# A hybrid RWKV/convolution block: a projection tile's products by halves of the contraction, not by quarters

## The chip, the cores and the metric

The kernel runs on one core of a Trainium2 chip. The metric is the device time of that core in microseconds for one execution. Lower is better. The engines are TensorE (PE in the profile; PEld is its loading of weights), VectorE (DVE), ScalarE (ACT), GpSimd (POOL) and SyncE (SP), which issues most transfers.

## The reference

One layer, one batch, 512 tokens of 2048 values with 16 meta tokens ahead of them:

```python
meta = jnp.broadcast_to(meta_tokens[None].astype(x.dtype), (bsz, N_META, D_MODEL))
h_res = jnp.concatenate([meta, x], axis=1)
hn = _rmsnorm(h_res, norm_in_g[l])
P = hn @ w_in[l]                        # (528 x 2048) @ (2048 x 8320)
Pr, Pc = P[..., :RW_COLS], P[..., RW_COLS:]
prev = jnp.pad(Pr[:, :-1], ((0, 0), (1, 0), (0, 0)))
Pr = Pr + (prev - Pr) * mu_shift[l]     # r, k, v, g_r and two narrow low-rank inputs
...
y = _rwkv7_recurrence(rh, decay, kh, vh, kk, kk * ah)   # 16 heads of 64, state carried over tokens
y_a = (yn + bonus) * jax.nn.silu(g_r)
Bg, Cg, hc, g_c = ...                   # four blocks of 1024 columns of Pc
y_b = Bg * _causal_depthwise_conv(Cg * hc, conv_w[l]) * jax.nn.silu(g_c)
h_res = h_res + jnp.concatenate([y_a, y_b], axis=-1) @ w_out[l]
out = _rmsnorm(h_res, norm_f_g)[:, N_META:]
```

The change concerns the first large product, `hn @ w_in`, alone.

## The kernel before, in words

**Tiles.** The projection is cut into 65 tiles of 128 output columns (`plan`). Each is a sum over 2048 rows, 16 blocks (`kt`) of 128. The first four tiles (`lora`, `k0`, `r0`, `B0`) are interleaved by a code of their own in `mains`; the other 61 are made one after the other by `main`. Their order is written out in `plan`, by pairs of head tiles: `k, r, v` of two neighbours, their `g`, and then one group `C, h, B, gc` of the convolution branch; from pair 4 on the order is the same, and the last four groups of the convolution branch come at the end, where the recurrence runs.

**Products.** All values are float32, split into a high and a low part of a shorter type. Each `kt` needs three products: high weight with low token part (`xl`), high weight with high token part (`xh`), and low weight with `xh`. A `B` or `gc` tile needs the 512 real tokens alone; it makes 48 products of 512 columns (`steps`). All others also need meta tokens: `k` and `v` tiles ("full") all 16, and `r`, `g`, `C`, `h` tiles ("tail") the last two. There the 512 tokens lie in two token pieces of 256, each in a PSUM bank of its own: the straight piece (r = 0) and the wide piece (r = 1). Copies of the meta tokens stand behind the real ones, and the wide piece reaches over them in its `xh` passes: a full tile's widths in the passes high·`xl`, high·`xh`, low·`xh` are 256, 288 and 274, a tail tile's 256, 260 and 258 (`WIDE`). That makes 96 products.

**Order inside a tile.** `pieces` (L343 to L356) goes by quarters of the contraction, four `kt` each: first the 12 straight products, `kt` by `kt`; then the 12 of the wide piece, pass by pass. The order of PE's instructions is that of the code; on the other engines a scheduler arranges them, with priorities (`ahead`, `high_priority`).

**Weights.** A tile's weights arrive in two transfers of 512 KB on SP's queue (`prefetch`, three raw buffers). Each is two quarters, and `split_w` makes the two parts of a quarter: a cast on ScalarE (L151) and a subtraction on VectorE (L152), "low part" below. The pool `hl` holds six quarters; a quarter's buffer is free for the next cast when the last product that reads it is done. `main` asks for two transfers a tile, one at its start and one ahead of the second quarter.

**Other work on PE.** The products of the recurrence's preparation (`prepare`, `invert`) and of the recurrence (`recur`) are put between projection products. `fill(ns)` lets the projection run on until its products have counted `ns`, and each product counts its width times 0.43. The same count (`clock`) releases deferred transfers (`later`, `run_pending`), SP's queue of stores and reloads among them. For a pair of heads, `prepare` makes the triangular products `gram` (L754) and, in `gram_meta`, a few narrow ones: key norms (L786), products with the meta tokens (L765) and, for the odd tile of a pair, the second level of a triangular inverse (`level_b`, L1023 and L1027). The narrow ones are written into the two PSUM banks of the projection tile that comes next (`next_banks`), ahead of its first product. VectorE empties them by two masks (L775) and eight copies (`take_b`, L1037), ScalarE by a copy of the norms. If the projection tile has counted more than 48 products at that point, `gram_meta` stands ahead of `gram`, otherwise behind it. In `invert`, the products `t0` (L961) read `xn`, a transpose (L946) on VectorE.

**Evictions.** At a tile's end VectorE scales its two banks into SBUF (`scaled`, L402, L403, L413), and ScalarE, VectorE and GpSimd finish it (shift by a token, gate, convolution).

Of the kernel before, what the change touches and what calls it, by code (L numbers as in the profile page):

```python
# [18 lines left out]
P = 128  # L19
DM = 2048  # L20
KT = DM // P
SEQ = 512
META = 16
# [66 lines left out]
def hymba_kernel(ctx: ExitStack, tc: tile.TileContext, xt, xtok, front, w_in, w_out, pv, lup, cst, msk, gf, out):  # L90
    nc = tc.nc
# [41 lines left out]
    quarters, chain, low = {}, {}, {}  # L133
    state = {"next": 0, "step": 0, "banks": []}
# [13 lines left out]
    def split_w(q, rq, eng):  # L148
        what, i, half = kind_of(q // 2)
        hi, lo = parts_of((what, i, half + q % 2), f"w{q}")  # L150
        nc.scalar.copy(hi, rq)  # L151
        low[q] = eng.tensor_tensor(out=lo, in0=rq, in1=hi.bitcast(F32), op=ALU.subtract).ins  # L152
        quarters[q] = (hi, lo)

    def prefetch(upto):
        while state["next"] < min(upto, len(stream) if chain else N_IN):
            j = state["next"]
            raw = chain[j - N_IN] if j >= N_IN else wp.tile([P, 1024], F32, tag="raw", name=f"wr{j}", bufs=3)
            state["dma"] = nc.sync.dma_start(raw, stream[j]).ins
            with tc.high_priority(offset=WEIGHTS):  # L160
                for q in range(2):
                    split_w(2 * j + q, raw[:, q * 512 : (q + 1) * 512], nc.vector)
            state["next"] = j + 1
# [6 lines left out]
    xh = xp.tile([P, KT, LX], F32R, name="xh")  # L170
    xl = xp.tile([P, KT, LX], F32R, name="xl")
# [159 lines left out]
    HALF, EX = META + SEQ // 2, 2 * META  # L331
    WIDE = {"full": (L + EX, L, L + META + 2), "tail": (L + 4, L, L + 2)}
# [7 lines left out]
            nc.scalar.copy(rsx[:, o : o + b - a], rs[:, a:b])  # L340
        nc.scalar.copy(rst, rsx[:, 0:4])

    def pieces(kind, ps, k4, q):  # L343
        hi, lo = quarters[q]
        for r in range(2):
            a = HALF if r else META
            ends = WIDE[kind] if r else (HALF,) * 3
            passes = ((hi, xl, ends[1]), (hi, xh, ends[0]), (lo, xh, ends[2]))
            for n, k in [(n, k) for n in range(3) for k in range(4)] if r else [(n, k) for k in range(4) for n in range(3)]:
                ww, xx, b = passes[n]  # L350
                kt = 4 * k4 + k
                nc.tensor.matmul(  # L352
                    ps[r][:, 0 : b - a], ww[:, k * P : (k + 1) * P], xx[:, kt, a:b], start=(kt == 0 and n == 0),
                    stop=(kt == KT - 1 and n == 2), skip_group_check=True,
                )
                yield (b - a) * 0.43  # L356

    def steps(ps, ranges, k4, q, ks=range(4), rs_=range(2)):
        hi, lo = quarters[q]
        for r, (a, b) in enumerate(ranges):  # L360
            if r not in rs_:
                continue
            for k in ks:
                kt = 4 * k4 + k
                w = slice(k * P, (k + 1) * P)
                for n, (ww, xx) in enumerate(((hi, xh), (hi, xl), (lo, xh))):
                    nc.tensor.matmul(  # L367
                        ps[r], ww[:, w], xx[:, kt, a:b], start=(kt == 0 and n == 0), stop=(kt == KT - 1 and n == 2)
                    )
                    yield (b - a) * 0.43  # L370

    def banks(ranges, name, pool, tag):
        return [pool.tile([P, b - a], F32, tag=tag, name=f"ps_{name}_{r}") for r, (a, b) in enumerate(ranges)]
# [5 lines left out]
    def main(j, ranges, name):  # L379
        prefetch(2 * j + 4)  # L380
        early = state["banks"]
        state.update(tile=j, step=0, banks=[])
        kind = ranges if isinstance(ranges, str) else None
        if kind:
            ranges = ((META, HALF), (HALF, WIDE[kind][0]))
        ps = [early[r][:, 0 : b - a] for r, (a, b) in enumerate(ranges)] if early else banks(ranges, name, pm, "main")
        for k4 in range(4):
            if k4 == 1:
                prefetch(2 * j + 5)
            for t in pieces(kind, ps, k4, 4 * j + k4) if kind else steps(ps, ranges, k4, 4 * j + k4):  # L390
                state["step"] += 1
                yield t
        return ps
# [149 lines left out]
    def mains():  # L543
# [35 lines left out]
        for j in range(4, len(plan)):  # L579
            what, i = plan[j]  # L580
            rg = "full" if what in ("k", "v") else REAL if what in ("B", "gc") else "tail"
            ps = yield from main(j, rg, f"{what}{i}")
            if (what, i) == ("h", 0):
                state["conv"] = low[4 * j + 6]
            if what == "gc" and i < 4:
                state["split"] = low[4 * j + 4]
            use(what, i, ps)
# [710 lines left out]
    for half in range(2):  # L1298
        units += [(half, "M1", g) for g in range(4)]
        units += [(half, prod, g) for g in range(4) for prod in ("P5", "M7", "M3", "Q6")]  # L1300
        ends = ("P4", 0), ("P4", 1), ("M2", 0), ("P4", 2), ("M2", 1), ("P4", 3), ("M2", 2), ("M2", 3)
# [156 lines left out]
    for half in range(2):  # L1458
        o = 28 * half
        for g in range(4):  # L1460
            b = o + 4 + 4 * g
# [51 lines left out]
    for u, unit in enumerate(units):  # L1513
        half, prod, g = unit
# [53 lines left out]
    with tc.manual_schedule(engines={mybir.EngineType.DVE, mybir.EngineType.Activation, mybir.EngineType.Pool}):  # L1568
# [15 lines left out]
        ends = [po.tile([P, 256], F32, tag="o", name=f"end{part}") for part in range(2)]  # L1584
        for part in range(2):
            cols = slice(256 * part, 256 * part + 256)
            for jj in range(8):
                hi, lo = right[(1, "M2", jj // 2), jj % 2]
# [75 lines left out]
```

## Time and profile before

| what | value |
|---|---|
| median of 3 runs | 993.13 us (991.97 to 993.62) |
| span of the profiled execution | 991.2 us |
| PE busy | 981.2 us, 99%, 9511 instructions |
| VectorE busy | 707.8 us, 71% |
| ScalarE busy | 390.4 us, 39% |
| GpSimd busy | 128.0 us, 13% |
| DMA, SP's main queue | 60.2% of 16 engines' span |
| moved | 176.89 MB, 178 GB/s over the span |
| TensorE's granted clock | full speed, 9 tenths or more in each of the 40 slices |

The page gives no time of its own for the profiled execution beside its span of 991.2 us. In the lists below a row has its start in us from the span's start, its duration in us, the engine, the line, the operation, output and inputs by the program's names without their numbers, the shapes, and how many instructions are merged into it; a bracket tells the idle time ahead of it and what ended that. Ends of products are modelled, starts are recorded. A row of the page's first two lists stands for the whole span.

### The profile page before, as it was taken

What the parts mean: (1) busy time and instruction counts of PE and PEld (TensorE: products, weight loads), DVE (VectorE), ACT (ScalarE), POOL (GpSimd) and SP (SyncE); (2) the same over time, 40 slices, a digit from 0 to 9 for tenths busy, and PEclk for the clock granted to TensorE, in tenths of its full rate; (3) what the DMA queues carried; (4) which work ended last, traced back from release to release, by engine and by line L of the source; (5) the groups of instructions that cost most, each with busy time, mean ns of one, the idle gap of its engine ahead of it and who ended that gap; (6) DMA issues with size and microseconds to landing.
All of it is one profiled execution on the core that took longest, in us unless ns stands there. A gap on an engine that the chain in (4) does not pass through costs nothing.

```text
span 991.2 us, 23393 instructions
## 1 busy us (share of the span) xinstructions
PE 981.2 (99%) x9511; PEld 907.4 (92%) x9511; DVE 707.8 (71%) x1413; ACT 390.4 (39%) x731; POOL 128.0 (13%) x242
## 2 busy tenths in 40 slices
PE   9999999999999999999999999999999999999996
PEld 8999999999998999998999998889889898788885
DVE  6777966578675679653779654465756697998897
ACT  7553432344322434322434323232332435546464
POOL 0110302012010121010111010011211102001001
PEclk9999999999999999999999999999999999999999
DMA  9526576246675385853375856988886697697654
GB/s 324 156 91 149 145 202 160 88 126 150 152 181 166 92 194 117 211 150 107 87 186 122 205 143 189 280 250 250 229 252 189 179 281 197 183 313 197 149 128 170
DMA packets 205387, 176.89 MB, mean 178 GB/s; under 512 B 138528, under 2 KB 168032, under 8 KB 204768
## 3 DMA queue, kind: packets, MB, share of 16 engines
q1 hardware_dynamic: 202688, 166.50, 60.2%
q0 software_dynamic: 2304, 8.39, 4.9%
q8 instruction: 74, 1.21, 0.5%
q10 hardware_dynamic: 288, 0.52, 0.1%
q14 instruction: 33, 0.27, 0.1%
HBM read 139.02 MB, written 36.35 MB: 177 GB/s over the span
## 4 chain that ended last, share of the span: by engine, by line
PE 94%; DVE 3%; DMA 1%; ACT 1%; issue 1%; SPq 0%; DVEq 0%; POOL 0%; ACTq 0%
PE ps_v L352 9%; PE ps_h L352 9%; PE ps_C L352 9%; PE ps_g L352 9%; PE ps_gc L367 9%; PE ps_B L367 9%; PE ps_k L352 8%; PE ps_r L352 8%; PE M L1381 5%; PE P L1381 4%; PE Q L1381 2%; PE g L754 2%; PE ps_lora L367 1%; PE ps_k L367 1%; PE zy L1139 1%; PE ps_r L367 1%
## 5 line engine op out<-in xcount | busy, mean ns | idle before, releaser
L151 ACT CAST w<-wr 128x512 fp32r<-128x512 f32 x252 | 153.7, 619 | 285.8 <-PE ps_C L352 47.5
L152 DVE TENSOR_TENSOR w<-wr,w 128x512 fp32r<-128x512 f32 x252 | 175.3, 707 | 117.7 <-ACT w L151 116.7
L352 PE MATMUL ps_v<-xh,w 128*128 128x256 f32 (+2 forms) x512 | 84.0, 285 | 0.0
L367 PE MATMUL ps_B<-xh,w 128*128 128x512 f32 x256 | 83.4, 394 | 0.0
L352 PE MATMUL ps_h<-xh,w 128*128 128x256 f32 (+2 forms) x512 | 81.6, 281 | 0.0
L352 PE MATMUL ps_g<-xh,w 128*128 128x256 f32 (+2 forms) x512 | 81.5, 281 | 0.0
L367 PE MATMUL ps_gc<-xh,w 128*128 128x512 f32 x256 | 81.1, 392 | 0.0
L352 PE MATMUL ps_C<-xh,w 128*128 128x256 f32 (+2 forms) x512 | 80.8, 280 | 0.0
L352 PEld LDWEIGHTS ps_v<-xh,w 128*128 128x128 f32 x512 | 73.9, 188 | 0.3
L352 PE MATMUL ps_k<-xh,w 128*128 128x256 f32 (+1 forms) x448 | 73.4, 285 | 0.0
L352 PE MATMUL ps_r<-xh,w 128*128 128x256 f32 (+1 forms) x448 | 72.6, 281 | 0.0
L352 PEld LDWEIGHTS ps_h<-xh,w 128*128 128x128 f32 x512 | 72.1, 189 | 0.3
L352 PEld LDWEIGHTS ps_g<-xh,w 128*128 128x128 f32 x512 | 72.0, 189 | 0.4
L352 PEld LDWEIGHTS ps_C<-xh,w 128*128 128x128 f32 x512 | 71.7, 189 | 0.2
L352 PEld LDWEIGHTS ps_k<-xh,w 128*128 128x128 f32 x448 | 64.7, 188 | 0.4
L352 PEld LDWEIGHTS ps_r<-xh,w 128*128 128x128 f32 x448 | 63.5, 189 | 0.2
L352 PE MATMUL ps_h<-xl,w 128*128 128x256 f32 x256 | 57.3, 281 | 0.0
L367 PEld LDWEIGHTS ps_gc<-xh,w 128*128 128x128 f32 x256 | 47.8, 188 | 10.0
L367 PEld LDWEIGHTS ps_B<-xh,w 128*128 128x128 f32 x256 | 47.8, 188 | 9.7
L352 PE MATMUL ps_C<-xl,w 128*128 128x256 f32 x256 | 56.2, 280 | 0.0
L352 PE MATMUL ps_v<-xl,w 128*128 128x256 f32 x256 | 55.8, 278 | 0.0
L352 PE MATMUL ps_g<-xl,w 128*128 128x256 f32 x256 | 55.5, 278 | 0.0
(382 smaller groups left out, 2143.6 us busy)
## 6 DMA issues: line engine op xcount, KB each, us to landing
wr<-in_w_in_dram SPq DMA_DIRECT2D x126, 512.0 KB
ct<-opd SPq DMA_DIRECT2D x72, 192.0 KB
wo<-in_w_out_dram SPq DMA_DIRECT2D x24, 512.0 KB
x<-in_w_out_dram POOLq DMA_DIRECT2D x16, 512.0 KB, 5.7
opd<-ar SPq DMA_DIRECT2D x8, 576.0 KB
opd<-gt SPq DMA_DIRECT2D x16, 288.0 KB
bd<-bt SPq DMA_DIRECT2D x64, 64.0 KB
bw<-bd SPq DMA_DIRECT2D x16, 256.0 KB
```

The lines of the kernel that those rows point to most:

```text
L151: nc.scalar.copy(hi, rq)
L152: low[q] = eng.tensor_tensor(out=lo, in0=rq, in1=hi.bitcast(F32), op=ALU.subtract).ins
L352: nc.tensor.matmul(ps[r][:, 0 : b - a], ww[:, k * P : (k + 1) * P], xx[:, kt, a:b], start=(kt == 0 and n == 0), stop=(kt == KT - 1 and n = ...
L367: nc.tensor.matmul(ps[r], ww[:, w], xx[:, kt, a:b], start=(kt == 0 and n == 0), stop=(kt == KT - 1 and n == 2))
L754: nc.tensor.matmul(z[h][:, c - c0], bk[hs, c, h : h + 2, :].rearrange("p a s -> p (a s)"), ar[hs, c].rearrange("p a s -> p (a s)"), start= ...
L1139: nc.tensor.matmul(zy[e][hs if e else ho, k], t[hs, o : o + CH], x, start=(n == 0), stop=(n == 2))
L1381: nc.tensor.matmul(bank[s], left(prod, jj, m, s), w, start=(jj == 0 and n == 0), stop=(jj == 7 and n == 2))
```

## The change

`pieces` now goes by halves of the contraction, eight `kt` each, and its argument is the half and the number of its first quarter. In the first half of a tile the wide piece comes first (passes high·`xh`, low·`xh`, high·`xl`, eight products each) and then the 24 straight products, `kt` by `kt`. In the second half the 24 straight products come first, and the wide piece last (passes high·`xl`, high·`xh`, low·`xh`). `main` asks for the tile's second transfer after the 24th product, where that was ahead of the second quarter, also after 24. The 96 products of a tile, their widths, operands and banks are the same. `steps`, for `B` and `gc`, is as before. Lines from 401 on have numbers that are higher by 10; L352 becomes L354.

```diff
-    def pieces(kind, ps, k4, q):
-        hi, lo = quarters[q]
-        for r in range(2):
-            a = HALF if r else META
-            ends = WIDE[kind] if r else (HALF,) * 3
-            passes = ((hi, xl, ends[1]), (hi, xh, ends[0]), (lo, xh, ends[2]))
-            for n, k in [(n, k) for n in range(3) for k in range(4)] if r else [(n, k) for k in range(4) for n in range(3)]:
-                ww, xx, b = passes[n]
-                kt = 4 * k4 + k
-                nc.tensor.matmul(
-                    ps[r][:, 0 : b - a], ww[:, k * P : (k + 1) * P], xx[:, kt, a:b], start=(kt == 0 and n == 0),
-                    stop=(kt == KT - 1 and n == 2), skip_group_check=True,
-                )
-                yield (b - a) * 0.43
+    def pieces(kind, ps, half, q0):
+        ks = range(8 * half, 8 * half + 8)
+        xs = ((0, xl), (0, xh), (1, xh))
+        ends = [META + b - HALF for b in (WIDE[kind][1], WIDE[kind][0], WIDE[kind][2])]
+        straight_, split_ = [(0, kt, n, SEQ // 2) for kt in ks for n in range(3)], []
+        for n in (0, 1, 2) if half else (1, 2, 0):
+            split_ += [(1, kt, n, ends[n] - META) for kt in ks]
+        for at_, (r, kt, n, w) in enumerate(straight_ + split_ if half else split_ + straight_):
+            part, xx = xs[n]
+            k, a = kt % 4, HALF if r else META
+            first = not half and at_ in (0, 24)
+            nc.tensor.matmul(
+                ps[r][:, 0:w], quarters[q0 + kt // 4][part][:, k * P : (k + 1) * P], xx[:, kt, a : a + w], start=first,
+                stop=half == 1 and at_ in (23, 47), skip_group_check=True,
+            )
+            yield w * 0.43
...
+        if kind:
+            for half in range(2):
+                for n, t in enumerate(pieces(kind, ps, half, 4 * j)):
+                    if not half and n == 24:
+                        prefetch(2 * j + 5)
+                    state["step"] += 1
+                    yield t
+            return ps
...
-            for t in pieces(kind, ps, k4, 4 * j + k4) if kind else steps(ps, ranges, k4, 4 * j + k4):
+            for t in steps(ps, ranges, k4, 4 * j + k4):
```

On PE, at the start of the tile `C2`, which follows `g5`. The two banks are `ps_C2_0` (straight) and `ps_C2_1` (wide); w130, w131 are the last two quarters of g5, w132 and w133 the first two of C2. Before:

```order
L352 MATMUL ps_g5_1_5342<-xh_114,w131_5279 128x260 x4
L352 MATMUL ps_g5_1_5342<-xh_114,w131_5279 128x258 x4
L352 MATMUL ps_C2_0_5687<-xl_115,w132_5311 128x256
L352 MATMUL ps_C2_0_5687<-xh_114,w132_5311 128x256 x2
...
L352 MATMUL ps_C2_1_5688<-xl_115,w132_5311 128x256 x4
L352 MATMUL ps_C2_1_5688<-xh_114,w132_5311 128x260 x4
L352 MATMUL ps_C2_1_5688<-xh_114,w132_5311 128x258 x4
L352 MATMUL ps_C2_0_5687<-xl_115,w133_5314 128x256
```

and after:

```order
L354 MATMUL ps_g5_1_5342<-xh_114,w131_5279 128x258 x4
L354 MATMUL ps_C2_1_5688<-xh_114,w132_5312 128x260 x4
L354 MATMUL ps_C2_1_5688<-xh_114,w133_5315 128x260 x4
L354 MATMUL ps_C2_1_5688<-xh_114,w132_5312 128x258 x4
L354 MATMUL ps_C2_1_5688<-xh_114,w133_5315 128x258 x4
L354 MATMUL ps_C2_1_5688<-xl_115,w132_5312 128x256 x4
L354 MATMUL ps_C2_1_5688<-xl_115,w133_5315 128x256 x4
L354 MATMUL ps_C2_0_5687<-xl_115,w132_5312 128x256
```

The wide products of the end of one tile and of the start of the next stand side by side now, and the first quarter of C2 is read up to its 36th product where it was read up to its 24th.

On PE, where the narrow products of head tile 3 (`sq3`, `ar3`, and `level_b` of pair 1 with `xT0`, `xo0`) stand. Before, behind five products of g3 and the `gram` products, in the banks of C1:

```order
L754 MATMUL g3_5_1_3494<-ar3_3114,bk3_3115 128x128
L786 MATMUL ps_C1_0_3511<-sq3_3293,cs_66 32x144 x4
L765 MATMUL ps_C1_0_3511<-ar3_3114,bk3_3115 128x16
L765 MATMUL ps_C1_1_3512<-ar3_3114,bk3_3115 128x16
L1023 MATMUL ps_C1_0_3511<-xT0_1304,tm0_0_2896 32x32 x2
...
L1027 MATMUL ps_C1_1_3512<-xo1_1906,tm0_1_2897 32x32 x2
L352 MATMUL ps_g3_0_3481<-xh_114,w80_3200 128x256
```

and after:

```order
L354 MATMUL ps_g2_1_3348<-xh_114,w79_3163 128x258
L796 MATMUL ps_g3_0_3460<-sq3_3286,cs_66 32x144 x4
L775 MATMUL ps_g3_0_3460<-ar3_3108,bk3_3109 128x16
L775 MATMUL ps_g3_1_3461<-ar3_3108,bk3_3109 128x16
L1033 MATMUL ps_g3_0_3460<-xT0_1303,tm0_0_2891 32x32 x2
...
L1037 MATMUL ps_g3_1_3461<-xo1_1902,tm0_1_2892 32x32 x2
L764 MATMUL g3_1_0_3511<-ar3_3108,bk3_3109 128x128
...
L764 MATMUL g3_5_1_3514<-ar3_3108,bk3_3109 128x128
L354 MATMUL ps_g2_1_3348<-xh_114,w79_3163 128x258 x3
L354 MATMUL ps_g3_1_3461<-xh_114,w80_3202 128x260 x4
```

The narrow products stand three projection products ahead of the end of g2 (93 of its 96 are made), in the banks of g3, which begins right behind `gram`.

On VectorE at the same place, before:

```order
L795 TENSOR_TENSOR gt3_3488<-g3_5_1_3494,cs_66 128x512
L441 SCALAR_TENSOR_TENSOR g2_3460<-th_r2_3470,g2_3460 128x512
L775 TENSOR_TENSOR gt3_3488<-ps_C1_0_3511,cs_66 128x16
L775 TENSOR_TENSOR gt3_3488<-ps_C1_1_3512,cs_66 128x16
L1037 COPY xT0_1304<-ps_C1_1_3512 32x4x32
...
L1037 COPY xT1_1905<-ps_C1_1_3512 32x4x32 x2
```

and after:

```order
L413 TENSOR_TENSOR pr_g2_3539<-ps_g2_0_3347,rs_116 128x256
L152 TENSOR_TENSOR w84_3379<-wr42_3377,w84_3379 128x512
L785 TENSOR_TENSOR gt3_3457<-ps_g3_0_3460,cs_66 128x16
L785 TENSOR_TENSOR gt3_3457<-ps_g3_1_3461,cs_66 128x16
L1047 COPY xT0_1303<-ps_g3_1_3461 32x4x32
...
L1047 COPY xT1_1901<-ps_g3_1_3461 32x4x32 x2
L805 TENSOR_TENSOR gt3_3457<-g3_1_0_3511,cs_66 128x512
```

The masks and copies stand behind the low part of w84 (the first quarter of C1) now and ahead of the masks of `gram`.

On PE in the tile k2, the third quarter of which is w54. Before:

```order
L352 MATMUL ps_k2_1_2237<-xh_114,w53_2050 128x274 x4
L352 MATMUL ps_k2_0_2236<-xl_115,w54_2150 128x256
L352 MATMUL ps_k2_0_2236<-xh_114,w54_2150 128x256 x2
...
L352 MATMUL ps_k2_1_2237<-xl_115,w54_2150 128x256
L961 MATMUL t0_0_2316<-xn0_2279,gt0_1161 64x32 x2
L961 MATMUL t0_1_2317<-xn0_2279,gt0_1161 64x32 x2
```

and after:

```order
L354 MATMUL ps_k2_0_2236<-xl_115,w53_2052 128x256
L354 MATMUL ps_k2_0_2236<-xh_114,w53_2052 128x256 x2
L354 MATMUL ps_k2_0_2236<-xl_115,w54_2150 128x256
...
L354 MATMUL ps_k2_0_2236<-xh_114,w54_2150 128x256 x2
L971 MATMUL t0_0_2312<-xn0_2274,gt0_1160 64x32 x2
L971 MATMUL t0_1_2313<-xn0_2274,gt0_1160 64x32 x2
```

The products `t0` stand behind 57 projection products of k2 where there were 61.

## The prediction

> **What bounds the kernel now.** I read the page's busy times first, then the chain that ended last, then the matrix engine's timeline inside single tiles, since only there do orders inside a tile show.
>
> ```profile
> PE 981.2 (99%) x9511; PEld 907.4 (92%) x9511; DVE 707.8 (71%) x1413; ACT 390.4 (39%) x731; POOL 128.0 (13%) x242
> PE 94%; DVE 3%; DMA 1%; ACT 1%; issue 1%; SPq 0%; DVEq 0%; POOL 0%; ACTq 0%
> ```
>
> TensorE (PE) is busy 99% of the span and is 94% of the chain. So two things count: what one product costs PE, and any new wait of PE. Nothing else reaches the end of this kernel. The chain in order of time gives whole tiles (start, us, what):
>
> ```profile
> 130.49 11.17 PE ps_C L352 x96
> 376.72 11.44 PE ps_v L352 x96
> 610.32 11.21 PE ps_C L352 x96
> ```
>
> 96 products make a tile. A tail tile (`ps_C`) takes 11.17 us, a full one (`ps_v`) 11.44, and a tail tile that follows a tile of 512-wide products 11.21.
>
> **The price of a change of width.** The timeline of PE in that first C tile (start us, us, merged products), from its first product on:
>
> ```profile
> 130.33 0.28 PE L352 MATMUL ps_C<-xl,w 128*128 128x256 f32 x1
> 130.69 0.28 PE L352 MATMUL ps_C<-xl,w 128*128 128x256 f32 x1
> ...
> 132.16 1.12 PE L352 MATMUL ps_C<-xh,w 128*128 128x260 f32 x8
> 133.12 0.28 PE L352 MATMUL ps_C<-xl,w 128*128 128x256 f32 x1
> ...
> 133.48 0.28 PE L352 MATMUL ps_C<-xl,w 128*128 128x256 f32 x1
> ```
>
> Starts are what counts, since ends are modelled. A quarter is 16 products of 256 columns (the narrow ones) and then 8 of 260 or 258 (the wide ones). The first three narrow ones take 0.36 us (130.33 to 130.69), 120 ns each; the next 13 take 1.47 (to 132.16), 113.1 ns each; the 8 wide ones 0.96 (to 133.12), 120 ns each; the three after them 0.36 again. So narrow products that follow wide ones start slow: 0.36 - 3 x 0.1133 = 0.02 us for each change from wide to narrow. The full tile shows the same:
>
> ```profile
> 376.56 0.28 PE L352 MATMUL ps_v<-xl,w 128*128 128x256 f32 x1
> 376.92 0.28 PE L352 MATMUL ps_v<-xl,w 128*128 128x256 f32 x1
> ...
> 378.39 1.19 PE L352 MATMUL ps_v<-xh,w 128*128 128x288 f32 x8
> 379.42 0.28 PE L352 MATMUL ps_v<-xl,w 128*128 128x256 f32 x1
> ```
>
> 0.36 for three, 1.47 for 13, and 1.03 for 8 wide ones (288 and 274 columns), 129 ns each. What wide products cost in a longer run is seen once, early in the kernel, in 12 products of 258 columns followed by 12 of 256:
>
> ```profile
> 47.11 0.28 PE L367 MATMUL ps_r<-xh,w 128*128 128x258 f32 x1
> ...
> 47.60 0.28 PE L367 MATMUL ps_r<-xl,w 128*128 128x258 f32 x1
> ...
> 48.44 0.40 PE L367 MATMUL ps_r<-xh,w 128*128 128x258 f32 x2
> ```
>
> The first eleven take 1.33 us, 120.9 ns each; the last seven of these 0.84, 120.0 each.
>
> **Part 1, fewer changes of width: a gain.** The change keeps all 96 products of a tile and their widths. It puts the 16 wide products of a half side by side, last in a tile and first in the next, so that a tile has one change from wide to narrow in place of four. Three go: 3 x 0.02 = 0.06 us for a tail tile, if wide products keep their 120.0 ns. If in a run of 32 they cost the 120.9 of the whole run, 32 x 0.9 ns = 0.03 are given back. I take the middle, 0.045, as neither row is nearer. 31 tail tiles (7 r and 8 each of g, C and h): 1.4 us, between 0.9 and 1.9. For 15 full tiles (7 k, 8 v) the removed changes are worth the same 0.06, but no row shows a long run of 288; with the same share of 0.9 in 120 taken from 129 ns, 32 x 1.0 = 0.03 go back: 0.03 x 15 = 0.45, between 0.1 and 0.9 us.
>
> A second gain lies behind 512-wide tiles:
>
> ```profile
> 609.93 0.39 PE L367 MATMUL ps_gc<-xh,w 128*128 128x512 f32 x1
> 610.16 0.28 PE L352 MATMUL ps_C<-xl,w 128*128 128x256 f32 x1
> ...
> 612.04 1.12 PE L352 MATMUL ps_C<-xh,w 128*128 128x260 f32 x8
> ```
>
> Here all 16 narrow products are slow: 1.88 us, 117.5 ns each, and only wide ones end that. (That is 16 x 4.2 = 0.07 against a usual quarter's 0.02: the 0.04 between 11.21 and 11.17.) Eight tiles follow a tile of 512 columns (v0, k2, k4, k6 and C4 to C7); with the wide piece first, narrow products never follow 512. At 0.05 each this is 0.4 us, between 0 (if the wide ones are slow there in their stead) and 0.5. Sum of part 1: 1.4 + 0.45 + 0.4 = 2.25 us, between 1.0 and 3.3.
>
> By the Trainium skill (TensorE: Matmul & The Clock Gate, Back-to-back issue gap) an isolated warm gap is N / 2.4 + 2.5 ns, 109 for 256 and 111 for 260 columns, with nothing for a change of width. The rows above differ, 113.1 and 120, and the row decides; by the page part 1 would be worth 0.
>
> **Part 2, other work lands elsewhere: PE waits.** Each product is charged by its width in the count that spaces out foreign work, so within a half the same count is reached at another product. Two places matter. In tile k2 the products `t0` stand after 57 products in place of 61. They need `xn`, a transpose on VectorE (DVE) behind the low part of a weight quarter, whose cast on ScalarE waits for PE:
>
> ```profile
> 169.61 0.62 ACT L151 CAST w<-wr 128x512 fp32r<-128x512 f32 x1 [1.89 <-PE ps_k L352]
> 170.26 0.69 DVE L152 TENSOR_TENSOR w<-wr,w 128x512 fp32r<-128x512 f32 x1 [0.59 <-ACT w L151]
> 170.87 0.70 DVE L946 STREAM_TRANSPOSE xn<-xT 128x512 f32<-128x512 f32 x1
> 169.35 0.28 PE L352 MATMUL ps_k<-xl,w 128*128 128x256 f32 x1
> 170.94 1.36 PE L961 MATMUL t<-xn,gt 64*64 64x32 f32 x64
> 171.61 0.03 issue
> ```
>
> PE frees that quarter with its 48th product, just ahead of 169.35, and the chain cast, low part, transpose ends at 171.57. PE now does 13 products and half of `t0` meanwhile and stands 0.03 us at 171.61: it is just in time. The second quarter is still freed by the 48th product, so the chain stays while PE arrives 4 products earlier: 4 x 113 ns = 0.45 us of wait, at least 0, at most 0.55.
>
> The second place is the boundary between g2 and g3. Now the level-b products and the meta products of pair 1 write C1's banks, a whole tile ahead of their use. With the change they write g3's banks, three products ahead of g3, and g3's first product needs bank 1 emptied: two masks and eight copies on DVE. These stand behind the low part of weight w84, whose buffer PE frees at product 92 of g2, one product before. Durations:
>
> ```profile
> 252.50 2.06 PE L754 MATMUL g<-ar,bk 64*128 64x128 f32 x32
> 254.48 0.45 PE L786 MATMUL ps_C<-sq,cs 128*32 128x144 f32 x8
> 255.90 0.38 PE L352 MATMUL ps_g<-xh,w 128*128 128x256 f32 x1
> 258.75 0.24 DVE L775 TENSOR_TENSOR gt<-ps_C,cs 128x16 f32<-128x16 f32 x2
> 258.92 2.37 DVE L1037 COPY xT<-ps_C 32x128 f32<-32x128 f32 x8
> ```
>
> PE's cover from product 92 on: one product 0.12, meta and level-b 1.42 (254.48 to 255.90), gram 1.98 (252.50 to 254.48), three products 0.36: 3.88 us. DVE's way: cast 0.65 (169.61 to 170.26 above), low part 0.61, masks 0.17, copies 2.37, some 0.1 for the first semaphore: 3.90. So the wait is 0 if DVE is idle then. It is behind its work in this stretch:
>
> ```profile
> 250.98 1.85 DVE L152 TENSOR_TENSOR w<-wr,w 128x512 fp32r<-128x512 f32 x3
> 252.75 0.42 DVE L403 TENSOR_TENSOR pr_g<-ps_g,rs 128x256 f32<-128x256 f32 x1
> 251.82 0.28 PE L352 MATMUL ps_g<-xl,w 128*128 128x256 f32 x1
> ```
>
> Ahead of the masks it has three low parts and an eviction, which at today's pace end at 252.8 + 0.3 = 253.1, about 0.7 later than product 92 (near 251.1) + 0.1 + 0.65 + 0.61 allows. Between 0 and 0.7 I take 0.4; if the eight copies queue behind more, 1.2 is the far end. Part 2: 0.85 us, between 0 and 1.75. The other places where a tile's banks are lent (r3, k5, k7) keep 24, 16 and 16 products and the gram's 1.98 us as cover, 16 x 129 ns + 1.98 = 4.0 us against masks and copies, and cost nothing.
>
> **Part 3, weights held longer: nothing.** A quarter's buffers are freed after products 36, 48, 92 and 96 of the tile in place of 24, 48, 72 and 96, at most 20 products or 2.3 us later, and the second quarter is needed 20 products earlier, another 2.3, the fourth 12. ScalarE's cast and DVE's low part wait behind that, and other work of ScalarE behind the cast. The smallest spare today:
>
> ```profile
> 291.68 0.73 ACT L486 ACTIVATE cv<-u,pvt 128x512 f32<-128x512 f32 x1 [10.42 <-POOL u L484]
> 292.31 2.17 ACT L151 CAST w<-wr 128x512 fp32r<-128x512 f32 x4
> 293.89 2.49 DVE L152 TENSOR_TENSOR w<-wr,w 128x512 fp32r<-128x512 f32 x4
> 294.67 0.62 PE L367 MATMUL ps_B<-xh,w 128*128 128x512 f32 x2
> ```
>
> The low part done at 294.6 is used two products after the quarter's first (294.9), near 295.4: 0.8 us to spare. But these casts wait behind `cv` for GpSimd, not for a buffer, and follow the end of the tile h1, which the change leaves; B1 is untouched. In k2 the third quarter's low part is the first of five:
>
> ```profile
> 166.57 3.09 DVE L152 TENSOR_TENSOR w<-wr,w 128x512 fp32r<-128x512 f32 x5
> ```
>
> It is done by 167.3 and first used at 169.35, 2.1 us later, and its place in the tile stays. If this cover is gone, B1 pays 2.3 - 0.8 = 1.5 us. SP's weight transfers, queued with GpSimd's and other stores behind raw buffers that are freed with the low parts, start up to 2.3 us later and lie far ahead of use. The evictions keep their number; bank 0 closes at product 72 in place of 84, which takes load from a tile's end.
>
> **Sum.** -2.25 + 0.85 = -1.4 us, against this execution's 991.2 us span. The times shown have a median of 993.13, 1.9 above that span, which I take as what lies around it, so 991.7.
>
> **The rivals.**
> *A larger gain.* All ends of part 1 and no wait at g3: -3.3 + 0.45 = -2.9, 990.3. The 120.0 ns of the long run speaks for it, the transition into wide runs (120.9) against.
> *No gain on PE.* The slow starts are only early stamps that a later product repays: 0 + 0.85, 994.0. The page's rule above gives this too. Against: the quarters' sums, 2.79 us (130.33 to 133.12), hold the excess.
> *Slower: narrow products stay slow.* After 512 columns they keep 117.5 ns until the width changes. If 32 wide ones leave PE in that state, each of the 64 x 46 = 2944 narrow products costs 4.2 ns more: 12.4 us, 1004; in a quarter of the tiles 3.1 us, 994.8. It decides from 3.4 us on, 1.2 ns per narrow product. Against: after the 12 of 258 the narrow ones recover within three.
> *Slower: weights late.* PE waits of B1's kind in more places: with B1's 1.5 and g3's far end 1.2, -2.25 + 0.45 + 1.2 + 1.5 = +0.9, 994.0; two more such places 997.
>
> **How the numbers follow.** About 0.2%, 2 us, is what a measurement of this kernel tells from no change. Forecast 0.50, at 991.7 with its own range 990.7 to 993.0 (faster 0.20, same 0.30); larger gain 0.15 (faster); no gain 0.12 (same 0.10, slower 0.02); narrow slow 0.12 (slower); weights late 0.11 (same 0.05, slower 0.06). Faster 0.35, same 0.45, slower 0.20. The range 990.0 to 995.2 leaves out the far parts of the last two.
>
> **What would show it.** Right: a C tile near 11.12 us in the chain, the same behind gc; three slow narrow starts once a tile; a wait of 0.45 us at `t0` and up to 0.7 at g3. Wrong: narrow products at 117 ns, wide ones over 121, or PE waits for `w` outside these two places.

## The result: slower by 0.4%

The changed kernel takes 996.20 us (median of 5 runs, 995.84 to 999.18), the kernel before 992.29 (median of 5). The ratio is 1.004, with a 95% interval of 1.0029 to 1.0051. The profiled execution of the changed kernel has a span of 994.1 us, 2.9 more than the 991.2 of before. The medians are 3.9 apart; what is read from the two traces accounts for the 2.9 alone.

The busy times and the chain of the changed kernel, as the page has them:

```profile
PE 984.2 (99%) x9511; PEld 910.9 (92%) x9511; DVE 704.5 (71%) x1413; ACT 388.0 (39%) x731; POOL 132.1 (13%) x242
PE 86%; DVE 8%; DMA 2%; ACT 2%; issue 1%; POOL 1%; DVEq 0%; SPq 0%; ACTq 0%
```

PE is busy for 984.2 us where it was 981.2, with the same 9511 products. The span less that is 9.9 us now and was 10.0. So the loss is in the products themselves; in sum PE stands still no longer. The share of PE in the chain fell because the chain leaves PE at a wait at 256 us (the tile g3, below) and runs through other engines back to 212 us; PE was at work there all the same. What PE waits for, in total, times and longest (us):

```profile
PE pwarm L202 <- DVE cold L199: 1.0, 1, 1.0
PE t L971 <- DVE xn L956: 0.5, 1, 0.5
PE M L1391 <- DVE o L1360: 0.3, 1, 0.3
PE ps_g L354 <- DVE xT L1047: 0.3, 1, 0.3
```

The first and the third were there before. The other two are the waits at `t0` and at g3. The chain in order of time shows whole tiles of the changed kernel:

```profile
129.81 11.39 PE ps_C L354 x96
178.27 11.11 PE ps_r L354 x96
378.07 11.69 PE ps_v L354 x96
463.70 11.69 PE ps_k L354 x96
614.00 11.11 PE ps_C L354 x96
```

The C tile that took 11.17 us takes 11.39, the v tile that took 11.44 takes 11.69. But the C tile behind a gc tile, which took 11.21, takes 11.11, and so does r2, which the chain of before has at 11.27:

```profile
178.02 11.27 PE ps_r L352 x96
```

There are two kinds of tiles now. Here is a slow one on the timeline of PE, the tile C2, with its first half's wide products, its narrow ones, and the wide ones of the second half:

```profile
416.43 2.09 PE L354 MATMUL ps_C<-xh,w 128*128 128x260 f32 x16
418.36 1.22 PE L354 MATMUL ps_C<-xl,w 128*128 128x256 f32 x9
...
424.95 1.11 PE L354 MATMUL ps_C<-xl,w 128*128 128x256 f32 x8
425.89 2.08 PE L354 MATMUL ps_C<-xh,w 128*128 128x260 f32 x16
```

64 narrow products lie between 418.36 and 425.89: 7.53 us, 117.7 ns each. And the fast C4, behind gc:

```profile
613.84 2.08 PE L354 MATMUL ps_C<-xh,w 128*128 128x260 f32 x16
615.76 0.97 PE L354 MATMUL ps_C<-xl,w 128*128 128x256 f32 x7
...
623.02 0.76 PE L354 MATMUL ps_C<-xh,w 128*128 128x260 f32 x5
```

Here the same 64 take 7.26 us, 113.4 each. The narrow products of these tiles keep one of two paces, 113.3 or 117.7 ns, from their first few on to the next wide ones. The wide run ahead costs about the same in both, 1.93 and 1.92 us for 16.

From the starts of all products in the two traces (each product's time is the distance to the next one's start, and products that are followed by other work are counted at the mean of their tile), the 46 tiles fall into two groups. 19 have a mean of over 116.5 ns for their narrow products: C0 to C3, h0 to h3, h7, g4, g5, g7, k3, k4, k6, v4 to v7. They take 4.01 us more than before, 0.21 each. The other 27 take 1.50 us less, though in some of them a part is slow (k2's first half, at 117.8 ns). With the two waits, 0.46 and 0.25 as the timeline below has them, that is 4.01 - 1.50 + 0.71 = 3.2 us against a difference of the spans of 2.9.

```profile
171.44 0.67 PE L971 MATMUL t<-xn,gt 64*64 64x32 f32 x32 [0.46 <-DVE xn L956]
256.01 0.84 PE L354 MATMUL ps_g<-xh,w 128*128 128x260 f32 x5 [0.25 <-DVE xT L1047]
```

The two groups go by neighbours. Where no other work falls into the run of wide products ahead, the narrow ones begin slow in each of the 11 tail tiles that follow a tail tile (g1, g5, g7, C1 to C3, h0 to h3, h7) and in 11 full tiles: v1 and v4 to v7 behind a tail tile, k3, k5 and k7 behind a full one, k2, k4 and k6 behind 512-wide products. They begin fast in the tail tiles behind a full one (r1, r3, g2, g4, g6) and behind 512-wide products (C4, C5, C7). Other work in the middle of a tile then turns some: g1, v1, k5 and k7 go on fast behind it, g4 slow.

### The profile page after: what moved, and what is told of

It reads as the page before. It is cut to its first block, busy times and chain, and to the rows that moved or that the text cites. A ratio compares the mean times of both kernels' runs of the same rounds, so it can differ in the third digit from the quotient of the medians.

```text
span 994.1 us, 23385 instructions
## 1 busy us (share of the span) xinstructions
PE 984.2 (99%) x9511; PEld 910.9 (92%) x9511; DVE 704.5 (71%) x1413; ACT 388.0 (39%) x731; POOL 132.1 (13%) x242
## 4 chain that ended last, share of the span: by engine, by line
PE 86%; DVE 8%; DMA 2%; ACT 2%; issue 1%; POOL 1%; DVEq 0%; SPq 0%; ACTq 0%
PE ps_h L354 9%; PE ps_C L354 9%; PE ps_B L369 9%; PE ps_gc L369 9%; PE ps_v L354 8%; PE ps_g L354 8%; PE ps_k L354 8%; PE ps_r L354 7%; PE M L1391 4%; PE P L1391 2%; DVE o L1360 2%; PE ps_k L369 1%; PE g L764 1%; PE ps_r L369 1%; PE ps_lora L369 1%
## 5 line engine op out<-in xcount | busy, mean ns | idle before, releaser
L151 ACT CAST w<-wr 128x512 fp32r<-128x512 f32 x252 | 149.8, 619 | 235.2 <-PE ps_C L354 48.7
L152 DVE TENSOR_TENSOR w<-wr,w 128x512 fp32r<-128x512 f32 x252 | 172.2, 707 | 78.8 <-ACT w L151 76.2
L354 PE MATMUL ps_v<-xh,w 128*128 128x256 f32 (+2 forms) x512 | 82.5, 286 | 0.0
L354 PE MATMUL ps_h<-xh,w 128*128 128x256 f32 (+2 forms) x512 | 80.7, 283 | 0.0
L354 PE MATMUL ps_C<-xh,w 128*128 128x256 f32 (+2 forms) x512 | 79.1, 281 | 0.0
L354 PE MATMUL ps_g<-xh,w 128*128 128x256 f32 (+2 forms) x512 | 78.6, 282 | 0.3 <-DVE xT L1047 0.3
L354 PEld LDWEIGHTS ps_v<-xh,w 128*128 128x128 f32 x512 | 73.6, 189 | 0.3
L354 PEld LDWEIGHTS ps_h<-xh,w 128*128 128x128 f32 x512 | 71.3, 189 | 0.5
L354 PEld LDWEIGHTS ps_C<-xh,w 128*128 128x128 f32 x512 | 71.0, 188 | 0.5
L354 PEld LDWEIGHTS ps_g<-xh,w 128*128 128x128 f32 x512 | 70.7, 189 | 0.8 <-issue 0.4
L354 PE MATMUL ps_k<-xh,w 128*128 128x256 f32 (+2 forms) x448 | 71.3, 286 | 0.0
L354 PE MATMUL ps_r<-xh,w 128*128 128x256 f32 (+2 forms) x448 | 69.8, 280 | 0.0
L354 PEld LDWEIGHTS ps_k<-xh,w 128*128 128x128 f32 x448 | 64.3, 189 | 0.4
L354 PEld LDWEIGHTS ps_r<-xh,w 128*128 128x128 f32 x448 | 62.4, 188 | 0.1
L354 PE MATMUL ps_h<-xl,w 128*128 128x256 f32 x256 | 52.3, 281 | 0.0
L354 PE MATMUL ps_C<-xl,w 128*128 128x256 f32 x256 | 52.1, 280 | 0.0
L354 PE MATMUL ps_v<-xl,w 128*128 128x256 f32 x256 | 52.1, 279 | 0.0
L354 PE MATMUL ps_g<-xl,w 128*128 128x256 f32 x256 | 52.0, 278 | 0.0
```

The lines of the kernel that those rows point to most:

```text
L354: nc.tensor.matmul(ps[r][:, 0:w], quarters[q0 + kt // 4][part][:, k * P : (k + 1) * P], xx[:, kt, a : a + w], start=first, stop=half == 1 ...
```

## The experiments

### The two parts of the change apart

The first run keeps the order of before and charges each product what the changed kernel charges at its place. Other work on PE then stands where it stands after the change.

```diff
+        w1, w0, w2 = (b - HALF for b in WIDE[kind])
+        paid = [w1] * 8 + [w2] * 8 + [w0] * 8 + [w0] * 24
+        if k4 >= 2:
+            paid = [w0] * 32 + [w1] * 8 + [w2] * 8
+        paid = iter(paid[24 * (k4 % 2) : 24 * (k4 % 2) + 24])
...
-                yield (b - a) * 0.43
+                yield next(paid) * 0.43
```

> The order of before inside a tile, but each product counts what the product at its place counts after the change, so that the other work lands where it lands after it. Theory A (the loss of 3.9 us is in the products of the tiles themselves, most of it in narrow products that stay at 117.7 ns in about half of the tiles): only the two waits of the trace after, 0.5 us at t0 and 0.3 at g3, are left, 992.3 + 0.8 = 993.1 us, and narrow products are back at 113.3 ns. Rival B (the loss comes from the other work's new places): 995.5 to 996.2.

Measured: 993.13 us against 992.91, ratio 1.0005 (0.9996 to 1.0014). Its waits and its tiles:

```profile
PE t L966 <- DVE xn L951: 0.5, 1, 0.5
129.60 11.16 PE ps_C L357 x96
376.18 11.44 PE ps_v L357 x96
```

No tile is slow. The wait at `t0` is there, the one at g3 isn't. In this order g3 begins with its straight piece, whose bank is not the last to be emptied; that this is why was not tried. The places of the other work thus explain 0.2 us of the loss, at most 1.4 by the interval, and rival B falls.

The second run is its counterpart, the order of the change with the charges of before. All runs after it keep those charges.

```diff
+        paid = ([SEQ // 2] * 12 + [ends[n] - META for n in range(3) for _ in range(4)]) * 2
...
-            yield w * 0.43
+            yield paid[at_] * 0.43
```

> The order of the change, with the counts of before, so that the other work lands where it landed before. Theory A: 996.2 less the two waits of 0.8 us, 995.4, no wait at t0 and g3, and narrow products at 117.7 ns in about half of the 46 tiles. Rival B: 992 or below.

Measured: 995.91 us against 992.91, ratio 1.0031 (1.0018 to 1.0044). Both waits are gone, and the tiles are those of the change:

```profile
129.72 11.38 PE ps_C L355 x96
377.28 11.70 PE ps_v L355 x96
613.23 11.11 PE ps_C L355 x96
```

22 of 46 tiles are slow. So it is the order that costs 3 us (1.8 to 4.4 by the interval), and theory A stands.

### What leaves the narrow products slow

A run of 32 wide products differs from those of before in two things: it is longer, and it goes by eights. The next run changes only the second.

```diff
-        for n in (0, 1, 2) if half else (1, 2, 0):
-            split_ += [(1, kt, n, ends[n] - META) for kt in ks]
+        xls = [(1, kt, 0, ends[0] - META) for kt in ks]
+        split_ = [(1, kt, n, ends[n] - META) for f in (0, 4) for n in (1, 2) for kt in ks[f : f + 4]]
+        split_ = xls + split_ if half else split_ + xls
```

> As the run with the order alone, but inside a half the wide products go by quarters: four of 260 or 288, four of 258 or 274, and the same again, as they went before the change; the runs stay 32 long. Theory A1 (what the last eight wide products are decides in which pace the narrow ones start): all narrow products at 113.3 ns but for the first three, some 989.5 to 990.5 us. A2 (the length of the run of wide products decides): as the run with the order alone, 995.4.

Measured: 991.51 us against 992.91, ratio 0.9984 (0.9975 to 0.9993): faster than before, though a little less than expected. The chain:

```profile
129.93 11.12 PE ps_C L356 x96
375.38 11.40 PE ps_v L356 x96
413.60 11.14 PE ps_C L356 x96
608.90 11.38 PE ps_C L356 x96
```

41 tiles have a fast mean, also most of those that were slow. On the timeline of C2 the narrow products end their slow start after four and go on at 113.3 ns (from 416.42 to 417.78, 1.36 us for 12):

```profile
413.44 2.10 PE L356 MATMUL ps_C<-xh,w 128*128 128x260 f32 x16
415.37 0.40 PE L356 MATMUL ps_C<-xl,w 128*128 128x256 f32 x2
...
416.42 0.39 PE L356 MATMUL ps_C<-xh,w 128*128 128x256 f32 x2
...
417.78 0.39 PE L356 MATMUL ps_C<-xh,w 128*128 128x256 f32 x2
```

The same 32 products, in another order, leave PE in the other pace; the length alone (A2) doesn't decide. Five tiles are slow: C4 and C7, which follow 512-wide products, h4 behind C4, and g4 and g5. In g4 the trace shows another way in: its narrow products are at 113 to 114 ns until other work interrupts them after the 25th product, and at 117 to 119 behind it.

The two wide passes in turned order:

```diff
-        for n in (0, 1, 2) if half else (1, 2, 0):
+        for n in (0, 2, 1) if half else (2, 1, 0):
```

> As the run with the order alone, but the wide low-weight pass (258 or 274) goes ahead of the wide high-weight pass (260 or 288) in both halves. A1: the narrow ones then follow eight products of 260 or 288; their pace can differ from that of the order alone, 990 if it is 113.3 everywhere, 998.5 if it is 117.7 everywhere. A2: as the order alone, 995.4.

Measured: 995.40 us against 992.91, ratio 1.0022 (1.0014 to 1.0031), with 16 slow tiles, and others than before:

```profile
130.49 11.11 PE ps_C L355 x96
141.60 11.39 PE ps_h L355 x96
377.81 11.41 PE ps_v L355 x96
462.96 11.70 PE ps_k L355 x96
```

v4 to v7 are fast, C0 too, while h0 and the k tiles behind 512-wide products stay slow. This run also has two waits of its own, 0.6 and 0.3 us, of the low-rank products for ScalarE. It can't be told from it alone what part of the order matters.

Runs of 16 wide products by eights, which start from narrow ones:

```diff
-        for n in (0, 1, 2) if half else (1, 2, 0):
+        for n in (0, 1, 2):
...
-        for at_, (r, kt, n, w) in enumerate(straight_ + split_ if half else split_ + straight_):
+        for at_, (r, kt, n, w) in enumerate(straight_ + split_):
```

> As the run with the order alone, but the straight piece comes first in both halves: runs of 16 wide products (eight and eight) that follow narrow ones, two changes back to narrow in a tile. If a run of 32 is needed for the slow pace, all narrow products recover within three or four: 46 x (0.06 - 0.03) = 1.2 us under before, 991.5. If eight and eight is enough, both narrow runs of undisturbed tiles stay at 117.7 ns: 64 x 4.2 = 0.27 us a tile, in half of the tiles as before 6 us over, 998, in all 1004.

Measured: 992.01 us against 992.62, ratio 0.999 (0.9981 to 0.9999).

```profile
129.61 11.12 PE ps_C L355 x96
312.93 11.56 PE ps_k L355 x96
609.18 11.26 PE ps_C L355 x96
```

Eight and eight that start from the fast pace leave the fast pace in undisturbed tiles: one tile of 46 (g3, which other work interrupts) is slow throughout. Behind 512-wide products the first half's 32 narrow ones are slow until the first wide run (k4 11.56, C4 11.26); half a tile is slow also in g0, k5, k7 and h4, each time behind an interruption by other work. So in undisturbed tail tiles that follow a tail tile neither by eights nor the run of 32 is slow by itself; both together are, as C1 and C2 of the changed kernel show. Behind another kind of tile they need not be: g2, behind a full tile, and C4, behind 512-wide products, are fast there with the same order.

A survey inside one kernel: five tiles that were slow with the order alone get another first half, all else stays.

```diff
+        turns = {
+            ("C", 0): [(n, f, f + 4) for f in (0, 4) for n in (1, 2)] + [(0, 0, 8)],
+            ("C", 1): [(n, f, f + 2) for f in (0, 2, 4, 6) for n in (1, 2)] + [(0, 0, 8)],
+            ("C", 2): [(2, 0, 8), (1, 0, 8), (0, 0, 8)],
+            ("C", 3): [(0, 0, 8), (1, 0, 8), (2, 0, 8)],
+            ("g", 5): [(n, f, f + 1) for f in range(8) for n in (1, 2)] + [(0, 0, 8)],
+        }.get(plan[q0 // 4], [(1, 0, 8), (2, 0, 8), (0, 0, 8)])
```

> As the run with the order alone, whose tiles C0 to C3 and g5 all stay slow (11.39 us, 117.8 ns a narrow product), but the first half's wide products go in another order in each of them: C0 by fours, C1 by twos, g5 one by one, C2 with 258 ahead of 260, C3 with the narrow pass of the wide piece ahead of both. If the order of the last wide products decides, C0 is fast (11.13 us) and others may be; if only the length of the run decides, C0, C1, C2 and g5 stay at 11.39 and C3, with eight narrow products between two runs of 16, is fast.

Measured: C0, C1, C2, C3 and an h tile that was left as it was, from the chain:

```profile
130.47 11.11 PE ps_C L362 x96
141.58 11.39 PE ps_h L362 x96
268.06 11.11 PE ps_C L362 x96
416.18 11.39 PE ps_C L362 x96
564.59 11.12 PE ps_C L362 x96
```

In turn, the tiles are fast by fours (C0), by twos (C1), one by one (g5, 11.09 us from its starts) and with eight narrow products between two runs of 16 (C3). With 258 ahead of 260 by eights (C2) the tile is slow. The h tiles behind the fast C tiles are slow again, since their own runs are those of the change. The time of this run, 995.01 us, is of no use beside the tiles.

### A version that beats both

By fours in general, by eights where 512-wide products went ahead of a tail tile:

```diff
+        by = 8 if kind == "tail" and not half and plan[q0 // 4 - 1][0] in ("B", "gc") else 4
-        split_ = [(1, kt, n, ends[n] - META) for f in (0, 4) for n in (1, 2) for kt in ks[f : f + 4]]
+        split_ = [(1, kt, n, ends[n] - META) for f in range(0, 8, by) for n in (1, 2) for kt in ks[f : f + by]]
```

> The run by fours, but in the four tail tiles behind a tile of 512-wide products (C4 to C7) the first half goes by eights, which left them fast (11.11 us) in the run with the order alone and in the changed kernel; by fours two of them and h4 were slow (11.37 to 11.39). If the pace is decided by the entry and the order: 3 x 0.25 = 0.75 us below the run by fours, 990.8; if other work or chance decides, no gain.

Measured: 990.96 us against 992.62, ratio 0.9984 (0.9975 to 0.9993). C4 and C7 are fast, h4 still isn't:

```profile
129.68 11.12 PE ps_C L357 x96
375.13 11.40 PE ps_v L357 x96
608.65 11.11 PE ps_C L357 x96
782.99 11.11 PE ps_C L357 x96
```

The times can't tell it from the run by fours, whose ratio is the same. In the starts of the products its 46 tiles sum to 0.53 us less.

One by one in all tiles (the loops of `n` and `kt` of the run by fours exchanged), and one by one in tail tiles with fours in full ones:

```diff
-        split_ = [(1, kt, n, ends[n] - META) for f in (0, 4) for n in (1, 2) for kt in ks[f : f + 4]]
+        split_ = [(1, kt, n, ends[n] - META) for kt in ks for n in (1, 2)]
```

> As the run by fours, but the wide products go one by one: 260 and 258 (288 and 274) in turn in all tiles. In the survey the tile g5 with this order took 11.094 us where by fours takes 11.13. If the pace depends on the order alone and this one always leaves the fast pace: tails 31 x 0.035 = 1.1 us below the run by fours, some 990 us; no trace shows this order with 288 and 274, so the 15 full tiles can gain as much or be slow (15 x 0.25 = 3.8, 994).

> One by one in tail tiles, by fours in full ones. If the pace is fast everywhere: 1.1 us below the run by fours, 990.2, and a tail tile of 11.10 us in the trace; if the entry from a full tile or from 512-wide products leaves it slow, some tiles stay at 11.37.

Measured: one by one in all tiles 990.94 us against 992.75, ratio 0.9978 (0.9969 to 0.9987), the lowest ratio of all, though its interval overlaps that of the run by fours; only v2 and g4 are slow. But its wide products are dearer, 121.5 ns in an undisturbed tail tile where by fours they are 120.5, so a C tile takes 11.15 and the expected gain over the run by fours isn't there:

```profile
413.34 11.15 PE ps_C L356 x96
```

The mixture of the two orders takes 991.93 us, ratio 0.9991 (0.9982 to 1.0001). Its tiles v4 to v7 are slow, and g0, though v tiles go by fours as in the third run:

```profile
376.64 11.71 PE ps_v L357 x96
```

For v4 to v7 only what went ahead differs: the r tile's last wide products went one by one. So the order of a run and the state in which it starts decide together.

## Why the prediction was wrong

**What bounds the kernel** was right. The kernel follows the busy time of PE, +3.0 us of it against +2.9 in the span.

**Part 1, fewer changes of width.** This step failed. It was priced at a gain of 2.25 us, on the assumption that narrow products behind any wide run start slow three times and then go at 113.3 ns. Where that held, the sizes were about right: by the starts, the 41 tiles with a fast mean in the run by fours gained 2.16 us. By fours an undisturbed tail tile gained 0.04 us (11.17 to 11.13) and the full tile v5 0.04 (11.44 to 11.40), where 0.045 and 0.03 were taken. In the changed kernel 27 tiles gained 1.50 us. But in 19 tiles the narrow products stayed at 117.7 ns, and these lost 4.01. Of that, 3.59 lies in narrow products and 0.45 in wide ones (the two are worked out apart from means, so that they sum to a little more).

The rival *narrow products stay slow* had that mechanism, its price (4.2 ns for each narrow product) and the figure from which it decides, with a chance of 0.12. Its sum for a quarter of the tiles was 994.8; with 19 of 46 tiles the same working gives 991.7 + 12.4 x 19 / 46 = 996.8, and 996.2 was measured. That 19 is known from the trace after alone; nothing in the prediction could give it. The evidence against it was that narrow products recover within three behind a run of 12 of 258 columns. That was one run in one order, and the trace of before held a second row that spoke for the rival: 16 narrow products at 117.5 behind 512 columns, with no recovery. The prediction put it down to the 512-wide products and read that "only wide ones end that". A third place in the same trace, the tile r2, contradicts both halves of that reading, and the prediction does not have it:

```profile
177.86 0.28 PE L352 MATMUL ps_r<-xl,w 128*128 128x256 f32 x1
179.74 1.13 PE L352 MATMUL ps_r<-xh,w 128*128 128x260 f32 x8
180.70 0.28 PE L352 MATMUL ps_r<-xl,w 128*128 128x256 f32 x1
182.59 1.12 PE L352 MATMUL ps_r<-xh,w 128*128 128x260 f32 x8
```

No 512-wide product stands next to r2; it follows the last eight wide products of k2, with other work ahead of those. Its first 16 narrow products take 1.88 us, 117.5 ns each, eight wide ones follow, and the next 16 take 1.89 again. So in the kernel before, wide products had already left the slow pace, and had not ended it. By the starts, 14 quarters of that trace have 16 uninterrupted narrow products at 117.6 to 118.1 ns: six behind 512 columns, seven behind a run of wide products with other work inside or beside it, and the second of r2. Two paces had been seen, and what sets them was not known. The step took the commoner one for the rule.

**Behind 512-wide tiles** the second gain was taken at 0.05 a tile. The tail tiles C4 and C7 gained 0.10 (11.21 to 11.11); k4 and k6 were slow (11.50 to 11.69 by their chain rows and starts), so in these full tiles the gain did not come: the narrow products no longer stand behind 512-wide ones, and are slow behind the 288- and 274-wide ones too.

**One gap or two.** The Trainium skill (TensorE: Matmul & The Clock Gate, Back-to-back issue gap) has an isolated warm gap of N / 2.4 + 2.5 ns, an estimate of 109 for 256 columns. The runs show two gaps, 113.3 and 117.7 ns, for the same instruction in the same kernel, so here too the rows decide.

**Part 2, waits.** 0.45 at `t0` was forecast, and 0.46 was measured (0.5 in the list of waits of the run with the charges alone). At g3, 0.4 between 0 and 0.7 was taken, and 0.25 measured. The step was right in both places and mechanisms.

**Part 3, weights held longer.** No wait for `w` appears among PE's waits, nor among those of the weight loads at L354, as forecast. That rival falls.

**The rivals of no gain on PE** and of a larger gain fall with the run by fours: the gain is real where the pace is kept, and 1.4 us in its medians, where part 1 was to give 2.25 and the larger gain 3.3. (That run has neither wait, so part 1 stands alone in it; by the starts its five slow tiles lose 0.85 us of what the 41 gain.)

The span of the forecast, 990.0 to 995.2, left out the far part of the rival that came.

## What to carry to other kernels

Where TensorE bounds a kernel and streams of equal products run at more than one pace in the trace, an order that changes what runs ahead of them is a bet on the pace, and the pace is worth more than the changes of width that one saves: here 0.27 us a tile against 0.04. Read start-to-start times of equal products tile by tile after every such change, and try several orders in different tiles of one kernel, since one profile then tells them all. Keep the placing of other work apart from the order when judging it, by holding the charges fixed.

## What the runs showed of the hardware

The same product of 256 columns goes at 113.3 or at 117.7 ns, start to start, and 64 of them in a row keep the pace they began with. Products of 512 columns, some runs of 32 wide products, and interruptions by other work (r2 before, g4 by fours) left the slower one; eight wide products between did not always end it (r2). It repeats: C2 took 11.387 us from its starts in the changed kernel and in the run with the order alone, and C1 11.173 in the kernel before and in the run with its order. The granted clock was 1.00 in both a slow and a fast tile:

```profile
130.30:141.68 11.38, 11.38 (x98) 11.38 (x98) 5.23 (x16) 3.47 (x7) 0.59 (x4) 1.00 0.92 227
613.83:624.93 11.10, 11.10 (x97) 11.09 (x96) 4.54 (x7) 2.72 (x5) 0.00 (x0) 1.00 0.83 259
```

(The columns are the stretch, the sum, the busy times of PE, weight loading, VectorE, ScalarE and GpSimd, the clock, and the DMA's share and GB/s.) So the clock isn't it. Nor do the other engines and the transfers sort these tiles: the fast one moves more, 259 GB/s against 227, and in the survey C0, C1 and C3 turned fast when only the order of products in five tiles changed. What inside PE keeps the pace stays open. The records of the weight loads, which run alongside the products, differ a little: in C2 about every third load beside its narrow products takes 192 ns and the others 187 or 188, in C4 all take 187 or 188. Whether that is a cause or a consequence isn't shown; no run here changed the loads or the sources of the operands.
